# A transformer block with an expert layer on one core: joined residual and norm, a square on ScalarE, half of the token matrices on GpSimd, and an earlier end of the mixing-in

## The chip, the cores and the metric

The kernel runs on one core of a Trainium2 chip, in one launch. The metric is the device time in microseconds. A core has five engines with queues of their own: TensorE (PE, matrix products into PSUM; PEld are its weight loads), VectorE (DVE), ScalarE (ACT), GpSimd (POOL) and SyncE (SP), which issues most DMAs. An engine runs its instructions in the order of its queue.

## The reference, cut to what matters

256 tokens of width 1024, all in f32, go through two blocks. Three places matter here: the two ends of sublayers in the first block, where a normed sum is added to x and x is normed again, and the expert layer of the second.

```python
# first block
x = x + _rms_norm(merged @ w_out[l], g_post_mix[l])
h2 = _rms_norm(x, g_pre_mlp[l])
m = jnp.square(jax.nn.relu(h2 @ w_up[l])) @ w_down[l]
x = x + _rms_norm(m, g_post_mlp[l])
# second block: starts with h = rms_norm(x, norm1_g); ends with
x = x + peer(rms_norm(x, norm2_g), w_query, sub_keys, expert_u, expert_v)
# peer, per token: 8 heads pick 16 of 16384 experts each, e = 128 * key1 + key2, with weight g
act = jax.nn.gelu(jnp.einsum('td,thkd->thk', xb, expert_u[e]))
out = jnp.einsum('thk,thkd->td', g * act, expert_v[e])
```

## The kernel before

Each f32 weight is split into two f32r parts, `wh` and `wl` (`weights`, L113): a DMA brings a piece of 1024 columns into `raw` (L110), ScalarE copies it to `wh` (L121), VectorE or GpSimd makes `wl = raw - wh` (L127). A product is three matmuls, hi x hi, hi x lo and lo x hi (`mm3`, L170). TensorE's order is that of the program (`in_line`, L143); on the other engines a planner sets the order of issue from its own estimate of the times. `cycle` (L100, L571, L606) says from which pool the buffers of the next piece come; `ring` stays open all through, `wkx` opens in space that the first attention leaves.

`rows_product` (L278) makes a sublayer's output for the two token blocks one after the other, in two PSUM tiles `pp` of 512 columns, and then calls `done`. At the end of the mixer that is `mixed` (L601), at the end of the MLP `mlp_done` (L636). Both call `residual` (L243) and `norm_parts` (L234). `residual`: ScalarE squares and sums `pp` (L212), ten small VectorE instructions make the inverse root (`rsqrt`, L192), VectorE makes `y = pp * r * gain` (L249) and adds it to `x` in SBUF (L250). `norm_parts` does the same on `x` (L212, L192, L240) and puts off the transposes of `y` (L151), which TensorE makes some products later, when `tick` says so; their results are split by ScalarE and VectorE (`split`, L178). While the second token block goes through this, TensorE works on the first block's part of the next sublayer.

In the MLP, `up_first` (L640, token-major, then transposed) and `up_done` (L612) apply the relu on ScalarE, square on VectorE (L615, L647) and split. `down` (L619) runs one unit after the other behind the up units.

The expert layer is computed densely: 64 units of `expert_u` (`u_unit`, L979) give `acts`, the gelu of all 16384 experts' products with all tokens (`u_done`, L969), and 64 units of `expert_v` (`v_units`, L1048) sum them up. In between each value is multiplied by its token's weight. For that, `weighted` (L998) makes for each token a 128 x 128 table: `m2` (L1025) has a 1 in row j, column key2 of pick j; `m1` (L1026) has the weight of pick j in column key1; TensorE multiplies them (L1007) into `acc`, and VectorE multiplies four tokens' tables into the activations that are there already (L1014, L1017); for units still to come ScalarE lays the table down in `acts` (L1019), and `u_done` multiplies it in (L976). `weighted` is a generator. It yields after every second token; TensorE gets a token's product when five tokens' matrices have been made. It is drawn once at each of the four steps of a unit, during units 32 to 63, that is 128 times; what is left is drawn behind the last unit (L1037 to L1042). Six buffers each hold `m1` and `m2`.

Of the kernel before, what the change touches and what calls it, by code (L numbers as in the profile page):

```python
# [9 lines left out]
F32 = mybir.dt.float32  # L10
# [3 lines left out]
AF = mybir.ActivationFunctionType  # L14
OP = mybir.AluOpType
# [4 lines left out]
P = 128  # L20
S = 256
TB = 2
D = 1024
KB = 8
# [52 lines left out]
def block_kernel(ctx: ExitStack, tc: tile.TileContext, a, out, dbg=None):  # L77
    nc = tc.nc
    vec, act, pe, pool = nc.vector, nc.scalar, nc.tensor, nc.gpsimd

    const = ctx.enter_context(tc.tile_pool(name="const", bufs=1))
    small = ctx.enter_context(tc.tile_pool(name="small", bufs=4))
# [70 lines left out]
    def defer(n, f):  # L153

        late.append([n, f])
# [20 lines left out]
    squared = [None]  # L176
# [31 lines left out]
    def rstd(srcs, junk, n):  # L208

        s = small.tile([P, 2], F32, name="ssq")  # L210
        for i, src in enumerate(srcs):
            squared[0] = act.activation(junk[:, i * 512:i * 512 + src.shape[1]], src, AF.Square, scale=float(n) ** -0.5,  # L212
                                        accum_out=s[:, i:i + 1])
        return rsqrt(s[:, 0:1], s[:, 1:2] if len(srcs) > 1 else 0.0)
# [25 lines left out]
            vec.scalar_tensor_tensor(y[:, c:e], src[:, c:e], r, gain[:, c:e], op0=OP.mult, op1=OP.mult)  # L240
        defer(wait, lambda: transpose_split(y[:, :n], n // P, dsth, dstl))

    def residual(wk, x, pp, gain):  # L243

        y = xp.tile([P, D], F32, name="ny", bufs=2)
        r = rstd(pp, y, D)
        for b in range(2):
            c = slice(b * 512, (b + 1) * 512)
            vec.scalar_tensor_tensor(y[:, c], pp[b], r, gain[:, c], op0=OP.mult, op1=OP.mult)  # L249
            vec.tensor_tensor(x[:, c], x[:, c], y[:, c], op=OP.add)  # L250


    def project(*args, **kw):
# [174 lines left out]
    hh, hl = parts()  # L428
# [139 lines left out]
    b1 = ExitStack()  # L568
    wkx = b1.enter_context(tc.tile_pool(name="wkx", bufs=1, reuse_waits="tile"))
    mixed_cycle = [wkx, ring] * 4  # L570
    cycle[:] = mixed_cycle  # L571


    mh, ml = parts()
# [24 lines left out]
    gpr = gain_row(wk, "g_pre_mlp", D)  # L599

    def mixed(tb, pp):  # L601
        residual(wk, x[tb], pp, gpm)
        norm_parts(wk, x[tb], D, gpr, hh[:, tb], hl[:, tb], 1 + tb)

    rows_product(mh, ml, "w_out", mixed)
    cycle[:] = [*mixed_cycle, wk, wk]  # L606
# [5 lines left out]
    def up_done(u, p):  # L612
        r = wk.tile([P, 2, S], F32, name="mr", bufs=3)
        act.activation(r, p, AF.Relu)
        vec.tensor_tensor(r, r, r, op=OP.mult)  # L615
        mf[u] = (wk.tile([P, 2, S], F32R, name="mfh", bufs=5), wk.tile([P, 2, S], F32R, name="mfl", bufs=5))
        split(r, *mf[u])

# [15 lines left out]
    hn, hnl = parts()  # L634

    def mlp_done(tb, pp):  # L636
        residual(wk, x[tb], pp, gpo)
        norm_parts(wk, x[tb], D, g_n1, hn[:, tb], hnl[:, tb], 1 + tb)

    def up_first(b):  # L640
        mf[2 * b], mf[2 * b + 1] = ([wk.tile([P, 2, S], F32R, name=n, bufs=5) for n in ("mfh", "mfl")] for _ in range(2))

        def emit(tb, p):
            t = slice(tb * P, (tb + 1) * P)
            r = wk.tile([P, 2, S], F32, name="mr", bufs=3).rearrange("p a b -> p (a b)")
            act.activation(r, p, AF.Relu)
            vec.tensor_tensor(r, r, r, op=OP.mult)  # L647

            def f():
                q = tps([P, 4, P])  # L650
                for k in range(4):
                    turn(q[:, k, :], r[:, k * P:(k + 1) * P])
                for n in range(2):
                    split(q[:, 2 * n:2 * n + 2, :], mf[2 * b + n][0][:, :, t], mf[2 * b + n][1][:, :, t])
            defer(1 if tb else 2 + b, f)
        return emit
# [3 lines left out]
    pp = None  # L660
# [337 lines left out]
    def weighted():  # L998
        ready = []
        banks = {}  # L1000

        def products(t, m1, m2):
            j = t // 4
            if t % 4 == 0:
                banks[j] = acc([P, 4, P])
            p = banks[j]
            matmul(p[:, t % 4, :], m2, m1, True, True)  # L1007
            if t % 4 < 3:
                return
            ts = slice(4 * j, 4 * j + 4)  # L1010
            k = 2 * (gelus[0] - HALF)
            pv = p.rearrange("p t c -> p c t")
            g = acts[0][:, :, ts]
            vec.tensor_tensor(g, g, pv[:, :P // 2, :], op=OP.mult)  # L1014
            if k:
                g = acts[1][:, :k, ts]
                vec.tensor_tensor(g, g, pv[:, P // 2:P // 2 + k, :], op=OP.mult)  # L1017
            if k < P // 2:
                act.activation(acts[1][:, k:, ts], pv[:, P // 2 + k:, :], AF.Copy)  # L1019
            mixed_in[0] = j + 1  # L1020

        for t in range(S):
            m1 = ab.tile([P, P], F32, name="m1", bufs=6)
            m2 = ab.tile([P, P], F32, name="m2", bufs=6)
            vec.tensor_scalar(m2, i128, key2[:, t:t + 1], None, op0=OP.is_equal)  # L1025
            vec.tensor_scalar(m1, i128, key1[:, t:t + 1], gwt[:, t:t + 1], op0=OP.is_equal, op1=OP.mult)  # L1026
            ready.append((t, m1, m2))
            if len(ready) > 4:
                products(*ready.pop(0))
            if t % 2:  # L1030
                yield
        while ready:
            products(*ready.pop(0))
            if len(ready) % 2 == 0:
                yield

    table = weighted()  # L1037
    for u in range(HALF, NU):
        for _ in u_unit(u):
            next(table, None)  # L1040
    for _ in table:
        pass  # L1042
    abs_.close()
# [128 lines left out]
```

## Time and profile before

| | us |
|---|---|
| median of 3 runs | 1353.45 (1352.4 to 1354.31) |
| the profiled execution | 1357.89 |
| its span | 1356.1 |
| mean granted clock of TensorE | 0.988 |

| engine | busy us | share of the span |
|---|---|---|
| PE | 1310.0 | 97% |
| PEld | 1166.8 | 86% |
| DVE | 979.8 | 72% |
| ACT | 667.1 | 49% |
| POOL | 197.8 | 15% |

| stretch, us | what runs |
|---|---|
| 0 to 160 | projections, two attentions, gates |
| 160 to 230 | w_branch, w_out, residual and norm |
| 230 to 435 | MLP, residual and norm |
| 435 to 545 | second block: projections, spatial gating, attention, w_out |
| 545 to 755 | queries; first 32 units of expert_u; the choice of experts beside them |
| 755 to 996 | last 32 units of expert_u, tokens mixed in |
| 996 to 1344 | 64 units of expert_v, final norm |

The busy shares are means over stages with different limits. TensorE's gaps are found in the timeline of its instructions: the figure in brackets is its idle time before the instruction and what ended it. Granted clock 1.00 is the upper of the clock's two levels (2.4 GHz), 0.50 the lower.

### The profile page before, as it was taken

Reading aid. Unit: us, or ns where it says so; the run is one execution under the profiler, and the core shown is the slowest. Engines: PE = TensorE matmul, PEld = TensorE weight load, DVE = VectorE, ACT = ScalarE, POOL = GpSimd, SP = SyncE. Lnnn points to the kernel's source line nnn. Section 1 sums busy time; section 2 is a strip of 40 time slices with the busy share of each in tenths; the row PEclk is TensorE's granted clock in tenths of the full one; section 3 lists DMA queues with packets and bytes.
Section 4 is the critical chain, followed back from the end, with each engine's and each line's share of the span. In section 5 each row is a group of like instructions: output and inputs, shape, how many; then the busy total and the mean of one; then the engine's idle time right before and its main releaser. Section 6 shows DMA issues by size and latency. Waiting matters only on the chain.

```text
span 1356.1 us, 22115 instructions
## 1 busy us (share of the span) xinstructions
PE 1310.0 (97%) x8324; PEld 1166.8 (86%) x8324; DVE 979.8 (72%) x2255; ACT 667.1 (49%) x1018; POOL 197.8 (15%) x103
## 2 busy tenths in 40 slices
PE   6999898999998999999999999999989999999997
PEld 5788896799986777999999999999978888888886
DVE  6676678555568795699995799999965555555555
ACT  5576644544444655455554444434434445444543
POOL 2221223322235235400000000000000000000001
PEclk9999898999998999999999999999989999999999
DMA  7453464666544424456666544444456666666662
GB/s 283 161 177 120 142 216 134 207 188 189 190 156 155 144 90 163 133 150 182 203 197 198 163 143 149 144 142 140 141 177 195 190 196 194 195 191 195 193 194 84
DMA packets 64187, 230.61 MB, mean 170 GB/s; under 512 B 7280, under 2 KB 7696, under 8 KB 63952
## 3 DMA queue, kind: packets, MB, share of 16 engines
q1 hardware_dynamic: 61632, 221.03, 52.6%
q0 software_dynamic: 1728, 6.07, 1.2%
q10 hardware_dynamic: 720, 2.10, 0.4%
q8 instruction: 65, 1.06, 0.3%
q14 instruction: 42, 0.34, 0.1%
HBM read 227.07 MB, written 2.10 MB: 169 GB/s over the span
## 4 chain that ended last, share of the span: by engine, by line
PE 80%; DVE 13%; issue 2%; ACT 2%; DMA 1%; SPq 0%; POOL 0%; ACTq 0%; DVEq 0%
PE acc L141 52%; PE mid L141 27%; DVE wl L127 4%; PE tps L151 2%; ACT wh L121 1%; DMA x<-in_x_dram 1%; DVE eq L902 1%; DVE ef L904 1%; PE tps L141 1%; DVE x L250 1%; DVE eq L899 1%; DVE at_s L346 1%; DVE tk_w L821 0%; DVE ny L240 0%; ACT ny L212 0%
## 5 line engine op out<-in xcount | busy, mean ns | idle before, releaser
L121 ACT ACTIVATE wh<-raw 128x1024 fp32r<-128x1024 f32 (+2 forms) x422 | 439.8, 1049 | 409.3 <-PE mid L141 197.6
L127 DVE TENSOR_TENSOR wl<-raw,wh 128x1024 fp32r<-128x1024 f32 (+1 forms) x350 | 449.4, 1287 | 211.6 <-ACT wh L121 211.3
L141 PE MATMUL mid<-hh,wh 128*128 128x256 f32 x1280 | 367.8, 287 | 0.0
L141 PE MATMUL mid<-hh,wl 128*128 128x256 f32 x1280 | 356.4, 278 | 0.8 <-DVE wl L127 0.8
L141 PE MATMUL mid<-hl,wh 128*128 128x256 f32 x1280 | 356.6, 279 | 0.0
L141 PEld LDWEIGHTS mid<-hl,wh 128*128 128x128 f32 x1280 | 242.5, 189 | 0.4
L141 PEld LDWEIGHTS mid<-hh,wh 128*128 128x128 f32 x1280 | 241.1, 188 | 0.4
L141 PEld LDWEIGHTS mid<-hh,wl 128*128 128x128 f32 x1280 | 240.4, 188 | 1.0 <-DVE wl L127 1.0
L127 POOL TENSOR_TENSOR wl<-raw,wh 128x1024 fp32r<-128x1024 f32 (+3 forms) x72 | 175.4, 2447 | 343.1 <-ACT wh L121 300.8
L141 PE MATMUL acc<-wh,ah 128*128 128x512 f32 x512 | 200.5, 392 | 2.9 <-ACT ah L179 2.9
L141 PE MATMUL acc<-wl,ah 128*128 128x512 f32 x512 | 200.1, 391 | 0.0
L141 PE MATMUL acc<-wh,al 128*128 128x512 f32 x512 | 200.1, 391 | 0.0
L141 PE MATMUL acc<-wh,hh 128*128 128x512 f32 (+2 forms) x288 | 117.2, 407 | 1.3 <-ACT hh L179 1.2
L141 PEld LDWEIGHTS acc<-wh,ah 128*128 128x128 f32 x512 | 96.8, 189 | 23.3 <-ACT ah L179 3.1
L141 PE MATMUL acc<-wh,hl 128*128 128x512 f32 (+2 forms) x288 | 114.4, 397 | 1.2 <-DVE hl L180 1.1
L141 PE MATMUL acc<-wl,hh 128*128 128x512 f32 (+2 forms) x288 | 114.1, 396 | 0.7 <-POOL wl L127 0.4
L141 PEld LDWEIGHTS acc<-wh,al 128*128 128x128 f32 x512 | 96.7, 189 | 20.3 <-DVE al L180 0.2
L141 PEld LDWEIGHTS acc<-wl,ah 128*128 128x128 f32 x512 | 96.8, 189 | 20.0
L1026 DVE TENSOR_SCALAR m<-tok,key,gwt 128x128 f32<-128x128 f32 x256 | 94.7, 372 | 0.0
L179 ACT ACTIVATE ah<-acts 128x512 fp32r<-128x512 f32 x64 | 40.4, 633 | 93.0 <-PE acc L141 88.9
L180 DVE TENSOR_TENSOR al<-acts,ah 128x512 fp32r<-128x512 f32 x64 | 44.3, 693 | 52.6 <-ACT ah L179 52.6
L1025 DVE TENSOR_SCALAR m<-tok,key 128x128 f32<-128x128 f32 x256 | 79.4, 311 | 3.8 <-PE acc L141 3.0
(259 smaller groups left out, 1721.4 us busy)
## 6 DMA issues: line engine op xcount, KB each, us to landing
raw<-in_expert_u_dram SPq DMA_DIRECT2D x128, 512.0 KB, 3.8
raw<-in_expert_v_dram SPq DMA_DIRECT2D x128, 512.0 KB, 4.4
raw<-in_w_down_dram SPq DMA_DIRECT2D x32, 512.0 KB, 4.3
raw<-in_w_up_dram SPq DMA_DIRECT2D x24, 512.0 KB, 4.5
raw<-in_w_in_dram SPq DMA_DIRECT2D x20, 512.0 KB, 4.5
raw<-in_w_gate_dram SPq DMA_DIRECT2D x16, 512.0 KB, 4.2
raw<-in_w_out_dram SPq DMA_DIRECT2D x16, 512.0 KB, 4.4
raw<-in_w_in_n_dram SPq DMA_DIRECT2D x12, 512.0 KB, 4.6
```

The lines of the kernel that those rows point to most:

```text
L121: i = act.activation(h[:, :n], raw[:, :n], AF.Copy)
L127: last_split[0] = eng.tensor_tensor(l[:, :n], raw[:, :n], h[:, :n].bitcast(F32), op=OP.subtract)
L141: in_line(pe.matmul(p, x, y, start=start, stop=stop))
L151: in_line(pe.transpose(out, src, ident))
L179: turned_[0] = act.activation(h, p, AF.Copy)
L180: vec.tensor_tensor(l, p, h.bitcast(F32), op=OP.subtract)
L250: vec.tensor_tensor(x[:, c], x[:, c], y[:, c], op=OP.add)
L346: vec.tensor_scalar(s[:, cols[tb]], s[:, cols[tb]], r[:, tb:tb + 1], None, op0=OP.mult)
L899: turn_of(vec.tensor_tensor(eq, i50.unsqueeze(1).unsqueeze(1).to_broadcast(shape), posf[:, h:h + 2, :].unsqueeze(3).to_broadcast(shape), o ...
L902: vec.tensor_tensor(eq, eq, ecand[:, h:h + 2, :].unsqueeze(2).to_broadcast(shape), op=OP.mult)
L1025: vec.tensor_scalar(m2, i128, key2[:, t:t + 1], None, op0=OP.is_equal)
L1026: vec.tensor_scalar(m1, i128, key1[:, t:t + 1], gwt[:, t:t + 1], op0=OP.is_equal, op1=OP.mult)
```

## The change

- `residual` and the `norm_parts` behind it become one function, `residual_norm`. It multiplies `pp` by the gain in PSUM, makes `pp = pp * r + x` there, squares and sums that, and makes the normed `y` from `pp` and the second gain. `x` is written last, by a ScalarE copy from PSUM.
- In the MLP the square of the relu is made by ScalarE.
- `cycle` for w_branch and w_out draws `ring, ring, wkx, wkx` in place of `wkx, ring`.
- `m2` is made by GpSimd, `m1` still by VectorE.
- At every twelfth step the generator is drawn a second time, so that it ends during unit 30 of these 32.

```diff
-    def residual(wk, x, pp, gain):
+    def residual_norm(x, pp, gain, gain2, dsth, dstl, wait):
         y = xp.tile([P, D], F32, name="ny", bufs=2)
-        r = rstd(pp, y, D)
+        cs = [slice(b * 512, (b + 1) * 512) for b in range(2)]
+        def square(s, b):
+            squared[0] = act.activation(y[:, cs[b]], pp[b], AF.Square, scale=float(D) ** -0.5, accum_out=s[:, b:b + 1])
+        s = small.tile([P, 2], F32, name="ssq")
+        square(s, 0)
+        vec.tensor_tensor(pp[0], pp[0], gain[:, cs[0]], op=OP.mult)
+        square(s, 1)
+        r = rsqrt(s[:, 0:1], s[:, 1:2])
+        vec.tensor_tensor(pp[1], pp[1], gain[:, cs[1]], op=OP.mult)
+        s = small.tile([P, 2], F32, name="ssq")
         for b in range(2):
-            c = slice(b * 512, (b + 1) * 512)
-            vec.scalar_tensor_tensor(y[:, c], pp[b], r, gain[:, c], op0=OP.mult, op1=OP.mult)
-            vec.tensor_tensor(x[:, c], x[:, c], y[:, c], op=OP.add)
+            vec.scalar_tensor_tensor(pp[b], pp[b], r, x[:, cs[b]], op0=OP.mult, op1=OP.add)
+            square(s, b)
+        r = rsqrt(s[:, 0:1], s[:, 1:2])
+        for b in range(2):
+            vec.scalar_tensor_tensor(y[:, cs[b]], pp[b], r, gain2[:, cs[b]], op0=OP.mult, op1=OP.mult)
+        defer(wait, lambda: transpose_split(y, KB, dsth, dstl))
+        for b in range(2):
+            act.activation(x[:, cs[b]], pp[b], AF.Copy)
...
-    cycle[:] = mixed_cycle
+    cycle[:] = [ring, ring, wkx, wkx] * 2
...
     def mixed(tb, pp):
-        residual(wk, x[tb], pp, gpm)
-        norm_parts(wk, x[tb], D, gpr, hh[:, tb], hl[:, tb], 1 + tb)
+        residual_norm(x[tb], pp, gpm, gpr, hh[:, tb], hl[:, tb], 1 + tb)
...
     def mlp_done(tb, pp):
-        residual(wk, x[tb], pp, gpo)
-        norm_parts(wk, x[tb], D, g_n1, hn[:, tb], hnl[:, tb], 1 + tb)
+        residual_norm(x[tb], pp, gpo, g_n1, hn[:, tb], hnl[:, tb], 1 + tb)
...
         act.activation(r, p, AF.Relu)
-        vec.tensor_tensor(r, r, r, op=OP.mult)
+        act.activation(r, r, AF.Square)
...
-            vec.tensor_scalar(m2, i128, key2[:, t:t + 1], None, op0=OP.is_equal)
+            pool.tensor_scalar(m2, i128, key2[:, t:t + 1], None, op0=OP.is_equal)
             vec.tensor_scalar(m1, i128, key1[:, t:t + 1], gwt[:, t:t + 1], op0=OP.is_equal, op1=OP.mult)
...
     table = weighted()
+    steps = 0
     for u in range(HALF, NU):
         for _ in u_unit(u):
             next(table, None)
+            steps += 1
+            if steps % 12 == 0:
+                next(table, None)
     for _ in table:
         pass
```

## Rows read from the trace of the kernel before

**Rows 1.** by stretch: length, then busy us of PE, PEld, DVE, ACT, POOL; clock
```profile
760.00:988.00 228.00, 228.00 (x1981) 228.00 (x1980) 224.22 (x703) 98.95 (x184) 0.00 (x0) 1.00 0.48 143
...
1000.00:1340.00 340.00, 340.00 (x1497) 281.45 (x1497) 194.98 (x186) 164.00 (x186) 0.00 (x0) 1.00 0.62 186
```

**Rows 2.** TensorE's timeline, mixer's end: start, us, instruction, idle before it
```profile
227.80 1.94 PE L151 MATMUL tps<-ident,ny 128*128 128x128 f32 x8 [4.92 <-DVE ny L240]
...
233.89 0.40 PE L141 MATMUL acc<-wl,hh 128*128 128x512 f32 x1
```

**Rows 3.** TensorE's timeline at the MLP's end
```profile
417.46 0.63 PE L151 MATMUL tps<-ident,cnat 128*128 128x128 f32 x4 [1.23 <-DVE rs_x L201]
419.92 1.29 PE L151 MATMUL tps<-ident,ny 128*128 128x128 f32 x8 [1.83 <-DVE ny L240]
...
423.09 0.80 PE L141 MATMUL acc<-wh,hl 128*128 128x512 f32 x1 [0.81 <-DVE hl L180]
...
428.35 0.39 PE L141 MATMUL acc<-wh,hl 128*128 128x512 f32 x1
```

**Rows 4.** TensorE's timeline at the first down product
```profile
248.17 0.50 PE L141 MATMUL acc<-wh,mfl 128*128 128x512 f32 x1 [2.23 <-DVE mfl L180]
```

**Rows 5.** TensorE's timeline at the passage from expert_u to expert_v
```profile
989.55 0.83 PE L141 MATMUL acc<-m,m 128*128 128x128 f32 x6
...
992.73 0.49 PE L141 MATMUL acc<-m,m 128*128 128x128 f32 x2 [1.10 <-DVE m L1026]
996.10 0.79 PE L141 MATMUL acc<-wh,ah 128*128 128x512 f32 x1 [2.88 <-ACT ah L179]
...
1001.79 0.40 PE L141 MATMUL acc<-wl,ah 128*128 128x512 f32 x1
```

**Rows 6.** VectorE's timeline at the mixer's end
```profile
214.85 0.93 DVE L250 TENSOR_TENSOR x<-x,ny 128x512 f32<-128x512 f32 x1
215.71 3.43 DVE L127 TENSOR_TENSOR wl<-raw,wh 128x1024 fp32r<-128x1024 f32 x1
219.06 2.89 DVE L250 TENSOR_TENSOR x<-x,ny 128x512 f32<-128x512 f32 x1
```

**Rows 7.** line L250: count, then shortest, median and longest ns
```profile
L250 DVE TENSOR_TENSOR x<-x,ny x8: 679/1203/2890, 204.1 to 412.3; 128x512 f32<-128x512 f32 x8
```

**Rows 8.** GpSimd's timeline at the mixer's end
```profile
212.81 8.59 POOL L127 TENSOR_TENSOR wl<-raw,wh 128x1024 fp32r<-128x1024 f32 x3 [7.79 <-ACT wh L121]
```

**Rows 9.** VectorE's timeline at the MLP's end
```profile
410.81 4.38 DVE L250 TENSOR_TENSOR x<-x,ny 128x512 f32<-128x512 f32 x2
```

**Rows 10.** TensorE's timeline at w_branch's first product
```profile
161.28 0.39 PE L141 MATMUL acc<-oah,wh 128*128 128x256 f32 x1 [3.66 <-ACT wh L121]
```

**Rows 11.** the chain that ended last, two tokens: start, us, what
```profile
788.78 0.44 PE acc L141 x4
```

**Rows 12.** VectorE's timeline with tokens, late
```profile
988.84 0.43 DVE L1025 TENSOR_SCALAR m<-tok,key 128x128 f32<-128x128 f32 x1
989.04 0.49 DVE L1026 TENSOR_SCALAR m<-tok,key,gwt 128x128 f32<-128x128 f32 x1
989.29 0.56 DVE L1014 TENSOR_TENSOR acts<-acts,acc 128x256 f32<-128x256 f32 x1
```

**Rows 13.** GpSimd's groups by shape: count, busy us, mean ns
```profile
L127 POOL TENSOR_TENSOR wl<-raw,wh 128x576 fp32r<-128x576 f32 x2 | 2.9, 1432 | 4.9 <-ACT wh L121 4.9
...
L127 POOL TENSOR_TENSOR wl<-raw,wh 128x384 fp32r<-128x384 f32 x2 | 2.0, 1019 | 13.6 <-ACT wh L121 7.0 <-PE acc L141 6.6
```

**Rows 14.** VectorE's timeline in the second attention
```profile
459.38 0.62 DVE L346 TENSOR_SCALAR at_s<-at_s,at_r 128x256 f32<-128x256 f32 x2
...
470.39 2.74 DVE L346 TENSOR_SCALAR at_s<-at_s,at_r 128x256 f32<-128x256 f32 x2
```

**Rows 15.** GpSimd's timeline in the second attention
```profile
470.33 2.39 POOL L127 TENSOR_TENSOR wl<-raw,wh 128x1024 fp32r<-128x1024 f32 x1 [2.78 <-ACT wh L121]
```

**Rows 16.** VectorE's groups, 752 to 990 us: count, busy us, mean ns
```profile
L127 DVE TENSOR_TENSOR wl<-raw,wh 128x1024 fp32r<-128x1024 f32 x65 | 81.0, 1246 | 6.0 <-ACT wh L121 6.0
```

More of the change, by code (lines that the diff above doesn't have):

```diff
@@ L646, in emit @@
             act.activation(r, p, AF.Relu)
-            vec.tensor_tensor(r, r, r, op=OP.mult)
+            act.activation(r, r, AF.Square)
             def f():
```

## The prediction

> **What bounds the kernel now.** I read the page first, by its busy shares and its chain that ended last: TensorE is busy 97% of the span and holds 80% of the chain, most of the rest is VectorE. So an edit that only unloads another engine buys nothing where TensorE has no gap, and the question is where it has gaps. I then read the busy time by stretch, and TensorE's timeline around each gap. The stretch in which tokens are mixed in (760 to 988 us) is full: TensorE is busy 228.00 of 228.00 us at granted clock 1.00, VectorE 224.22, GpSimd nothing [rows 1]. The reader should see that taking work from VectorE shortens nothing there by itself; it can matter only at the stretch's end. The gaps that the edits touch are four: the end of the mixer's residual, 4.92 us [rows 2]; the end of the MLP's residual, three waits of 3.87 us in all [rows 3]; the first down product, 2.23 us [rows 4]; and the passage from the last expert_u unit to the first expert_v unit, 989.55 to 996.10 [rows 5]. A long gap also costs clock: behind the first, ten products of 512 columns take from 229.74 to 233.89 [rows 2], 0.41 us each, where the expert_v stretch at granted clock 1.00 has 1497 in 340.00 us, 0.23 each [rows 1]. That is the lower of the clock's two levels, 1.2 GHz in place of 2.4.
>
> **The change part by part.**
>
> *The join at the mixer's end.* The second token block's path from its sum to its transposes leaves TensorE open for 4.92 us. On it the join removes the two additions into x (L250): 0.93 and 2.89 us [rows 6]. Alone such an addition takes 0.68 [rows 7]; these are long because both inputs lie in SBUF while GpSimd runs three splits (8.59 us) [rows 8], to which I come back below. It puts in two multiplications by the gain, of the same width, so 2 x 0.68 us, though one fits ahead of the inverse root. So 3.82 - 1.36 = 2.5 us come off, and 2.4 stay open. The low clock costs 4.15 us for ten products that need 2.30, thus 1.85, and an estimated 0.6 of the 1.94 us of the transposes [rows 2]. Whether the clock still falls after 2.4 us no row decides: I count half, 1.2. That makes **-3.7 us**. Ends: -7.2, 4.92 + 2.45 but for a rest, if the split at 215.71 (3.43 us in VectorE's queue [rows 6]) falls elsewhere too; -1.5, if VectorE's order puts more splits ahead of the new steps. The copy of x moves to ScalarE behind the norm, which idles there. The accumulators are held some steps longer, but the next product that takes one stands behind transposes that wait for the same norm, so that hides it; if it fails, it costs tenths.
>
> *The join at the MLP's end.* The same edit. Here the two additions take 4.38 us [rows 9], so 3.0 come off. TensorE waits 1.23, 1.83 and 0.81 us [rows 3]; the first wait is for a rotation that stands behind the additions in VectorE's queue, so it goes as well. About 0.8 us stay: next late is the split behind the transposes. From 423.09 to 428.35 twelve products take 5.26 us where 2.76 are needed, 2.5 us of clock [rows 3]. Together 3.1 + 2.5 = 5.6; I take **-5.5 us**, between -7 and -2.
>
> *The square on ScalarE* (L615, L647). Sixteen passes of 512 columns leave VectorE. Nearly all are made two units before TensorE needs them, so nothing there. Only the wait of 2.23 us [rows 4] hangs on VectorE's order: one pass leaves its queue, 0.68 us by the row of the same width [rows 7]. **-0.6 us**, between -2.2 and +1.0 (ScalarE late instead, one weight copy ahead of the square).
>
> *The order of buffers* (`cycle`, L571). 42 pieces have been drawn before w_branch, so its first piece falls on the pool wkx under both orders, and TensorE waited for that piece: 3.66 us at 161.28 [rows 10]. The second piece now falls there too, but is needed only 24 products later. **0**, with -3 and +2.5 as ends: the wait shrinks or grows by what the issue order on ScalarE does to that copy.
>
> *30 units in place of 32.* TensorE's work is the same. It drew two tokens at each of 128 steps; now there are ten draws more. The generator ends after 130, at step 120, so two units stand between the last token and the first expert_v product. Before, six tokens are open behind the last expert_u product (three at 989.55, the last at 992.73), and the first expert_v product starts at 996.10, behind a wait of 1.10 for m and one of 2.88 for the split of the weights; the thirteen products from there run mostly at the low clock, until 1001.79 [rows 5]. Without that, six tokens take 6 x 0.22 = 1.3 us [rows 11], the first product starts at 990.9 and the fourteenth at 990.9 + 13 x 0.23 = 993.9 in place of 1001.79: 7.9 us. I take **-7.3 us**, leaving 0.6 for a hitch; ends -7.9 and -4.
>
> *One factor on GpSimd* (L1025). VectorE loses 256 x 0.20 us (start to start) [rows 12]. GpSimd gets 256 instructions in a stretch where it has none [rows 1]; its DMA issues for the final stage come behind them as they now come behind the last expert_u product. Each m2 waits for a free buffer of six, and TensorE needs it five tokens later. What must it not exceed? 1981 products in 228.00 us [rows 1], 64 to a unit with eight tokens, are 7.37 us per unit; 0.67 tokens more, at 0.22 [rows 11], make 7.5, or 0.86 us per token. No row shows this operation on GpSimd. Its two-input passes took 1.02 us for 384 columns and 1.43 for 576 [rows 13]: 2.15 ns per column and 0.19 fixed, so 0.47 us at 128 columns. Ends: 0.19, the fixed part alone, and 1.02, the nearest larger row. I take 0.47, the line through those rows, high rather than low, since there is one input only. GpSimd is then 55% busy, and the term is **0**; its end below is 0 too, since TensorE has no gap to give back.
>
> Against that speaks what the rows show of the two engines together. VectorE's pass with a scalar operand, SBUF to SBUF (L346), took 0.62 us for two, but 2.74 when GpSimd had begun an operation of 2.39 us just before: it ended behind GpSimd's [rows 14, 15]. The Trainium skill states this as a rule (SBUF — State Buffer, Who interferes with whom): GpSimd shares one pair of ports with VectorE's two-port modes and two-input passes, and who comes first locks it for a whole instruction. By that rule, the trace agrees, m1 (L1026) and the splits of expert_u now exclude m2.
>
> In rows: m1 takes 0.25 us start to start [rows 12], and the splits 2 x 1.25 us [rows 16] per 8.67 tokens, 0.29; with d for m2, a token needs d + 0.54 of what they share, if changes of hand overlap nothing. At the mixer's end GpSimd's three splits of 2.39 and the two VectorE passes between them (0.68 and 1.25 alone) took 8.59, not 9.10 [rows 7, 8, 15, 16]: a change of hand overlaps 0.25 us, which leaves d + 0.29. The limit of 0.86 is reached at d = 0.57 with the overlap, at 0.32 without. With 0.47 and the overlap it is 0.76. I expect VectorE to lose to these waits about what it gains, and TensorE to stay the bound.
>
> The Trainium skill (GPSIMD Engine Reference, 4.1 Engine selection) has GpSimd at roughly line rate for one input. By it and the fixed part, d is an estimated 0.30 us, and the sum would be the same.
>
> **The sum.** -3.7 - 5.5 - 0.6 + 0 - 7.3 + 0 = -17.1 us. The profiled execution took 1357.89 us, 1.79 of them outside its span of 1356.1; nothing outside changes, so it would take 1340.8. It lies 0.33% above the median of the three runs shown, 1353.45, from which I forecast **1336.4 us**.
>
> **The rivals.**
> (a) *The joins pay little, the passage pays.* VectorE's queue is filled in an order of its own, and splits can come in front of the new steps; then each join gives its lower end. For it: 3.43 us of split stood there [rows 6]. Against: the additions themselves are gone. -1.5 - 2 - 7.3, about 1342.7.
> (b) *GpSimd and VectorE shut each other out.* The place is the stretch with tokens, the mechanism the lock above, the point 0.86 us per token. With d = 0.47 and no overlap: 0.47 + 0.54 = 1.01, so 256 x 0.15 = 38 us more, less the 17.1: 1374, slower than before. For it: VectorE is busy 224.22 of 228.00 us [rows 1], so waits there count, and L346. Against: the overlap in the rows, VectorE's relief of 0.20 us per token, and that tokens come in pairs between which GpSimd waits for buffers.
> (c) *The passage doesn't close.* The tokens end two units earlier, but the split of the first weights (2.88 us now [rows 5]) still stands behind the last unit's gelu on ScalarE, and two thirds of the gap stay. The joins pay: about 1341.2.
> (d) *Nothing arrives*: what the seams gain is lost as waits of TensorE for m2; 1352.
>
> **How the numbers follow.** Forecast 0.52, (a) 0.17, (c) 0.11, (b) 0.14, (d) 0.06. About 0.2% (2.7 us) is what a measurement of this kernel can tell from no change. Faster: forecast, (a) and (c), less 0.01: 0.79. Same: (d) and that 0.01: 0.07. Slower: (b), 0.14. The range may leave out 2 in 10: (b) stays outside, with (d). Its low end is every gain at its end but the buffers' luck only in part, near 1328; its high end takes in (a) with 0 to 6 us of waits at the lock, 1349.
>
> **What would show it.** Right: TensorE's wait ahead of the transposes is about 2.4 us at the mixer's end and under 1 at the MLP's; the new passes take 0.7 us whatever GpSimd does; the first expert_v product follows the last expert_u product within 0.6 us, at the full clock; m2 lasts 0.3 to 0.5 us on GpSimd, a unit 7.5. Wrong: units longer than 7.5 us, TensorE waiting there for m2 or a split, L1026 far above its 0.25 (b); splits of 3 us inside the joins' path (a); a wait for the weights' split at the passage (c).

## The result

| | before | changed |
|---|---|---|
| median, us | 1353.64 (1352.4 to 1354.31, 4 runs) | 1334.16 (1332.48 to 1335.88, 4 runs) |
| ratio of the two | | 0.9857 (95%: 0.984 to 0.9874), 19.4 us less |
| the profiled execution, its span, us | 1357.89, 1356.1 | 1335.88, 1334.1 |
| mean granted clock | 0.988 | 0.995 |

The forecast was 1336.4, so the time fell as far as forecast, and 2.2 us further. The parts of the sum did not all come from where they were expected, as the trace shows. The page of the changed kernel, its busy line and the engines' shares of the chain that ended last:

```profile
PE 1300.8 (98%) x8324; PEld 1159.9 (87%) x8324; DVE 908.5 (68%) x1983; ACT 683.5 (51%) x1042; POOL 407.7 (31%) x359
...
PE 88%; DVE 6%; issue 3%; ACT 1%; DMA 1%; POOL 1%; SPq 0%; POOLq 0%; ACTq 0%; DVEq 0%
```

TensorE is busy 9.2 us less, though it makes the same products: at the lower clock a product is longer, and from 545 to 744 us the products of before follow one another more slowly, as the last section shows. Its share of the chain rises from 80% to 88%.

TensorE's timeline of the changed kernel at the places of rows 10, 2, 4, 3 and 5 (start, us, instruction, idle before it and what ended it):

```profile
158.83 0.39 PE L141 MATMUL acc<-oah,wh 128*128 128x256 f32 x1 [1.42 <-ACT wh L121]
...
208.87 0.50 PE L141 MATMUL acc<-wh,hh 128*128 128x512 f32 x1 [1.26 <-ACT hh L179]
...
220.83 1.03 PE L151 MATMUL tps<-ident,ny 128*128 128x128 f32 x8
222.17 0.50 PE L141 MATMUL acc<-wh,hh 128*128 128x512 f32 x1 [0.30 <-ACT hh L179]
...
237.86 0.50 PE L141 MATMUL acc<-wh,mfl 128*128 128x512 f32 x1 [0.98 <-DVE mfl L180]
...
394.57 0.50 PE L141 MATMUL acc<-wh,hh 128*128 128x512 f32 x1 [0.76 <-ACT hh L179]
...
407.41 0.63 PE L151 MATMUL tps<-ident,ny 128*128 128x128 f32 x4 [0.44 <-DVE ny L264]
409.09 0.66 PE L151 MATMUL tps<-ident,ny 128*128 128x128 f32 x4 [1.06 <-ACT qT L410]
...
976.88 0.40 PE L141 MATMUL acc<-wh,ah 128*128 128x512 f32 x1
...
979.84 0.39 PE L141 MATMUL acc<-wl,ah 128*128 128x512 f32 x1
```

Read each row against the same product of before. At w_branch's first product the changed kernel is 161.28 - 158.83 = 2.45 us ahead [rows 10], at the first down product 248.17 - 237.86 = 10.31 [rows 4], at the first expert_v product 996.10 - 976.88 = 19.22, and at the fourteenth 1001.79 - 979.84 = 21.95 [rows 5]; from there on it is constant. These leads are the ledger of the whole study: every run below was laid beside before product by product, and "a stretch gives x" means that the lead grows by x over it.

| stretch | term of the prediction | changed kernel | parts alone |
|---|---|---|---|
| start to w_out (206) | order, 0 | 2.9, of it 0.5 before the change begins | e2: 3.0, of it 0.6 as well; untouched kernels 0.4 to 2.5 |
| w_out to the down products (206 to 260) | join -3.7, square -0.6 | 7.4 | joins: 3.1 (e1), 3.4 (e5); square: 1.2 (e10), with the joins 4.0 |
| MLP's end (400 to 440) | join -5.5 | 4.1 | 4.1 (e1, e5) |
| 440 to 545 | none | 1.6 lost | 0 (e1, e5) |
| 545 to 744 | none | 2.0 | 0.7 to 3.2 in the twelve other kernels, none of which touches it |
| 744 to the fourteenth expert_v product | units and m2, -7.3 | 7.3 | both: 8.2 (e3); units: 5.1 (e4); m2: 4.4 (e9); untouched kernels 0 to 0.8 |
| sum | -17.1 | 22.0 | |

The line 545 to 744 is not the change's. The profiled execution of before made its products there at a slightly slower pace, as the section at the end shows; its 1357.89 us lies above every other run of that kernel. It is 4.25 us above the median of before, and the profiled execution of the changed kernel is 1.72 above its own, which is about what the line 440 to 545 lost. The difference of the two, 2.5, is why the spans give 22.0 us and the medians 19.5. Each trace is one execution, and the last column says how far untouched kernels differ, so a single line is known to a microsecond or two.

### The profile page after: what moved, and what is told of

It is laid out like the page before. It is cut to its first block, busy times and chain, and to the rows that moved or that the text cites. A ratio compares the mean times of both kernels' runs of the same rounds, so it can differ in the third digit from the quotient of the medians.

```text
span 1334.1 us, 22359 instructions
## 1 busy us (share of the span) xinstructions
PE 1300.8 (98%) x8324; PEld 1159.9 (87%) x8324; DVE 908.5 (68%) x1983; ACT 683.5 (51%) x1042; POOL 407.7 (31%) x359
## 4 chain that ended last, share of the span: by engine, by line
PE 88%; DVE 6%; issue 3%; ACT 1%; DMA 1%; POOL 1%; SPq 0%; POOLq 0%; ACTq 0%; DVEq 0%
PE acc L141 51%; PE mid L141 35%; DVE wl L127 2%; PE tps L151 2%; DMA x<-in_x_dram 1%; POOL wl L127 1%; PE tps L141 1%; ACT wh L121 0%; DVE ma L605 0%; DVE rope_t L334 0%; DVE at_s L363 0%; DVE cnat L336 0%; DVE ny L240 0%; DVE hl L180 0%; DVE rope_t L335 0%
## 5 line engine op out<-in xcount | busy, mean ns | idle before, releaser
L1040 POOL TENSOR_SCALAR m<-tok,key 128x128 f32<-128x128 f32 x256 | 208.8, 831 | 211.0 <-ACT key L938 121.6
L1099 POOL TENSOR_TENSOR hh<-hh,hl 128x512 f32<-128x512 f32 x4 | 5.1, 1286 | 344.9 <-ACT hl L1098 344.9
L1041 DVE TENSOR_SCALAR m<-tok,key,gwt 128x128 f32<-128x128 f32 x256 | 84.3, 356 | 31.5 <-PE acc L141 31.5
```

Source lines behind the costliest of these rows:

```text
L1040: pool.tensor_scalar(m2, i128, key2[:, t:t + 1], None, op0=OP.is_equal)
L1099: pool.tensor_tensor(y[:, tb, c], y[:, tb, c], gfin[:, c], op=OP.mult)
```

## The experiments

**The joins alone (e1).** The kernel before with `residual_norm` in place of `residual` and `norm_parts`, nothing else.

> The kernel before, with the two joins alone. Theory S, read off the trace after: the joins stand by themselves. The MLP's first product starts about 7 us earlier (its 4.92 us of idle and the low clock behind it are gone), the second block's first attention product another 2.5 us, not 5.5, since the copies of x on ScalarE now stand ahead of splits; 9.5 us less in all, 1344. Theory P, the prediction's sizes: 3.7 us at the mixer's end and 5.5 at the MLP's, 9.2 in all, 1344 as well, but split the other way. Rival L: the mixer's end gained 7 only because another order of buffers had put other splits into VectorE's queue; alone it gains 2 to 4, and the whole 4.5 to 6.5, 1347 to 1349.

Measured: 1347.71 us, ratio 0.9944 (0.9929 to 0.996), 7.6 us less; the medians alone, against 1353.67 for before, give 6.0. In the trace it gives 3.1 us at the mixer's end and 4.1 at the MLP's. The prediction's 3.7 and 5.5 are nearer than theory S's 7 and 2.5: four microseconds at the mixer's end must come from another part. L's time is met; whether the order of buffers is the cause, as it says, e5 decides.

**The order of buffers alone (e2).**

```diff
-    cycle[:] = mixed_cycle
+    cycle[:] = [ring, ring, wkx, wkx] * 2
```

> The kernel before, with the other order of buffers for w_branch and w_out alone. Theory S: the wait of 3.66 us for w_branch's first split weights shrinks to about 1.4 us, and TensorE keeps its clock behind it, since one weight copy no longer blocks ScalarE ahead of the gates; 5 us less by the third w_branch unit, of which about half is given back at waits for splits in w_branch and w_out: 2 to 3 us less at the mixer's end, and in all 1351. Theory P, the prediction's: 0, within 1 us. Rival: the shorter wait came from the joins or from chance in the arrival of a transfer, and the wait is 3 us or more here too.

Measured: 1353.97 us, ratio 1.0004 (0.9995 to 1.0012): nothing. Three rows of TensorE's timeline show where the shorter wait goes:

```profile
158.67 0.39 PE L141 MATMUL acc<-oah,wh 128*128 128x256 f32 x1 [1.42 <-ACT wh L121]
...
169.52 0.38 PE L141 MATMUL acc<-oah,wh 128*128 128x256 f32 x1 [1.17 <-DVE ma L586]
...
208.13 1.32 PE L151 MATMUL tps<-ident,ny 128*128 128x128 f32 x8 [1.52 <-DVE ny L240]
```

The wait of 3.66 us [rows 10] is down to 1.42 here too, so it was not chance. The lead over before grows to 5.6 us by 169, and two waits of a length that before does not have there, 1.17 and 1.52 us, take most of it again: 2.3 us are left at the down products, no more than untouched kernels have there (1.7 to 3.2). Theory S had the shorter wait right and the total wrong; the prediction had the total right, though its lower end of -3 did come about for a while.

**m2 on GpSimd and 30 units (e3), 30 units with m2 on VectorE (e4), m2 on GpSimd with 32 units (e9).** They split the token part in two.

> The kernel before, with m2 on GpSimd and 30 units, the joins, the square and the order of buffers as before. Theory S and the prediction's steps alike: 7.3 to 7.9 us less, all of it at the passage from the last expert_u unit to the first expert_v unit, whose first products run at the full clock; TensorE is busy all through the stretch with tokens; 1346. Rival: the tokens cost some tenths of a us per unit by waits for m2, which the joins' earlier start had hidden; 3 to 5 us less, 1349 to 1350.

> The kernel before, with 30 units in place of 32 and m2 still on VectorE. It asks whether GpSimd's help was needed. VectorE is busy 224.2 us of 228 in the stretch with tokens; 30 units ask it for the same work in 15 us less. Theory N, needed: VectorE falls behind, by up to 224 - 213 = 11 us, TensorE waits for matrices or for the split of weights and loses what the passage gains, or more; between 3 us less and 4 us more than before. Theory U, not needed: the work that VectorE has there beside tokens (the splits of weights and activations) moves past the end of the tokens, where VectorE has two units of room, so the passage closes all the same and 6 to 8 us come off, as with GpSimd.

> The kernel before, with m2 on GpSimd alone, in 32 units. With 30 units the helper was worth 3.1 us in the trace (e3 against e4), by TensorE's waits for matrices of VectorE. Theory Z: in 32 units TensorE is full all the same, and at the passage it waits for the split of the first weights, which stands behind the last gelu and not behind matrices; 0, within 1.5 us of the kernel before, and the passage keeps its wait of 2.9 us. Rival W: VectorE, freed of 0.20 us per token, is ahead at the passage, the waits of 0.30 and 1.10 us for matrices go, and 2 to 3 us come off.

Measured, in times: e3 1343.58 us, 0.9927 (0.9913 to 0.9942), 9.9 less; e4 1348.73, 0.9962 (0.9948 to 0.9977), 5.1 less; e9 1349.86, 0.997 (0.9957 to 0.9982), 4.1 less. In the trace e3 gives 8.2 us over the passage, so its rival of 3 to 5 falls. TensorE's waits for VectorE in e4, inside the stretch with tokens, and its wait at the passage in e9:

```profile
932.84 0.49 PE L141 MATMUL acc<-m,m 128*128 128x128 f32 x2 [0.49 <-DVE m L1026]
954.48 0.49 PE L141 MATMUL acc<-m,m 128*128 128x128 f32 x2 [0.51 <-DVE m L1026]
959.19 0.49 PE L141 MATMUL acc<-m,m 128*128 128x128 f32 x2 [0.58 <-DVE m L1026]
```

```profile
990.11 0.50 PE L141 MATMUL acc<-wh,ah 128*128 128x512 f32 x1 [2.34 <-ACT ah L179]
```

With 30 units on VectorE alone the passage closes as well, but VectorE cannot keep up with eight tokens a unit: three waits, 1.58 us, and products of late tokens around them that follow one another more slowly. Beside e3 it loses 3.1 us in the stretch. Between theories N and U it lies nearer to U. With m2 on GpSimd and 32 units the waits of 0.30 and 1.10 us for matrices at the passage are gone and 2.34 of the 2.88 us stay [rows 5], so rival W is right: GpSimd pays by itself, at the passage, not in the stretch. Its 2 to 3 us were too few, since it left out the clock, which stayed at its upper level behind the 2.34 us. The first expert_v products (length, busy us of PE, PEld, DVE, ACT, POOL, granted clock), before and then e9:

```profile
996.00:1002.00 6.00, 5.90 (x14) 4.60 (x15) 1.29 (x2) 0.94 (x3) 0.00 (x0) 0.52 0.57 216
```

```profile
990.00:996.00 6.00, 5.83 (x24) 4.54 (x25) 2.68 (x4) 1.64 (x3) 0.00 (x0) 1.00 0.78 312
```

Of the 5.0 us that e9 gains over the passage itself, 1.9 are idle time, 0.8 the last tokens' products, and 2.3 this clock. In the times the two edits add up, 5.1 and 4.1 alone and 9.9 together, within intervals of about two microseconds each way; in the traces 5.1 and 4.4 alone stand against 8.2.

**The square back on VectorE in the changed kernel (e5), the square on ScalarE alone (e10).**

```diff
-        act.activation(r, r, AF.Square)
+        vec.tensor_tensor(r, r, r, op=OP.mult)
```

> The changed kernel, with the square of the MLP's relu back on VectorE. The joins alone (e1) took 3.1 us off around the mixer's end, where the changed kernel takes 7.4 off. Theory Y: the difference is the square. With it on VectorE the transposes and the first MLP products wait 0.37 and 0.89 us, the first down product 2.2 us in place of 0.98, and the clock falls behind that wait, 1.5 us more; so 3 to 4.5 us more than the changed kernel, 1337 to 1339. Theory P, the prediction's: the square is worth 0.6 us, 1335. Rival O: the difference is the order of buffers, which e1 did not have; then this kernel keeps the whole 7.4 but for 0.6, 1335 too, and the first down product waits 1 to 1.6 us without loss of clock.

> The kernel before, with the square on ScalarE alone. In the changed kernel it was worth 4.0 us around the mixer's end by the trace (against e5). Theory Y: that worth hangs on the joins. Alone, the 4.92 us ahead of the transposes stay and so does the low clock behind them; only the wait of 2.23 us at the first down product shrinks to about 1; 1 to 1.5 us less, 1352. Rival A: the parts add, and 3.5 to 4 us come off alone too, 1349.5. Theory P, the prediction's term: 0.6 us less, and nothing at the transposes.

Measured: e5 1336.04 us, 0.9863 (0.9846 to 0.9879); e10 1352.93, 0.9996 (0.9986 to 1.0006). The medians of e5 and the changed kernel are 1.9 us apart, and their runs overlap; the traces, one execution each, show where they differ. Between w_out and the down products e5 gives 3.4 us, the changed kernel 7.4, though e5 has the new order of buffers: rival O falls. TensorE's waits in e5 are e1's own, as theory Y said, and the long VectorE row below is the reason for the first two. TensorE, then VectorE in e5:

```profile
221.25 1.28 PE L151 MATMUL tps<-ident,ny 128*128 128x128 f32 x8 [0.37 <-DVE ny L264]
223.42 0.50 PE L141 MATMUL acc<-wh,hh 128*128 128x512 f32 x1 [0.89 <-ACT hh L179]
...
240.42 0.80 PE L141 MATMUL acc<-wh,mfl 128*128 128x512 f32 x1 [2.19 <-DVE mfl L180]
```

```profile
217.49 0.14 DVE L203 TENSOR_SCALAR rs_z<-rs_y 128x1 f32<-128x1 f32 x1
217.55 2.40 DVE L662 TENSOR_TENSOR mr<-mr 128x512 f32<-128x512 f32 x1
219.87 0.20 DVE L204 TENSOR_SCALAR rs_t<-rs_t 128x1 f32<-128x1 f32 x1
```

The square stands between two steps of the join's own inverse root, and there it lasts 2.40 us, not 0.68: both its inputs lie in SBUF, and GpSimd runs four splits from 210.23 on (11.95 us). This is rows 6 over again, in a new place. In the kernel before no square stood in that inverse root. Alone (e10) the edit left the wait ahead of the transposes at 5.47 us (4.92 in rows 2) and only shortened the one at the first down product to 0.98, as theory Y said; in the trace that is 1.2 us, in the times 0.6, which the interval does not tell from nothing.

With the joins the four microseconds are of three kinds: 1.4 at the transposes and the wait behind them, 1.2 for the shorter wait at the first down product (0.98 in place of 2.19), and 1.4 of clock behind that wait. For in e1 and e5 the clock, which no longer falls at the transposes, falls here, where before kept it behind the same wait of 2.23 us [rows 4]. The products behind that wait, before and then e5:

```profile
248.00:252.00 4.00, 3.83 (x17) 3.11 (x18) 0.54 (x2) 1.45 (x2) 1.42 (x1) 1.00 0.85 307
```

```profile
240.00:244.00 4.00, 3.58 (x10) 2.89 (x11) 0.79 (x3) 1.44 (x2) 0.28 (x1) 0.57 0.97 384
```

So the square is worth about a microsecond without the joins and four with them, by these traces. Whether the clock falls there in every execution was not measured.

**Where the copy of x goes: on VectorE (e6), on ScalarE but behind the splits (e12).**

```diff
-            act.activation(x[:, cs[b]], pp[b], AF.Copy)
+            vec.tensor_copy(x[:, cs[b]], pp[b])
```

```diff
-        defer(wait, lambda: transpose_split(y, KB, dsth, dstl))
-        for b in range(2):
-            act.activation(x[:, cs[b]], pp[b], AF.Copy)
+        def turned():
+            transpose_split(y, KB, dsth, dstl)
+            for b in range(2):
+                after(turned_[0], act.activation(x[:, cs[b]], pp[b], AF.Copy))
+        defer(wait, turned)
```

> The changed kernel, with the copy of x back to SBUF made by VectorE in place of ScalarE, right behind the normed y. Theory X: what the MLP's join failed to give (4.1 us in place of 5.5), and the new waits at both joins for ScalarE's splits (1.26 and 0.30 us at the mixer's end; 0.76, 0.34 and 1.06 at the MLP's), come from these copies, which stand ahead of the splits and of a rotation's copy in ScalarE's queue. Without them 2 to 3 us come off, 1331 to 1332. Rival V: the copies delay VectorE's own half of the splits and the second token block's chain by their 1.4 us; then the waits move to VectorE and the time stays within 1 us of the changed kernel, or grows by up to 2.

> The changed kernel, with the copies of x still on ScalarE but issued behind the splits of the transposes, not behind the normed y. It takes up again what e6 left open: whether the copies' place is what costs, without moving work to VectorE. Theory X: at the mixer's end the wait of 1.26 us falls to about 0.4 (as in e6) and the 0.30 goes; at the MLP's end 0.76 and 0.34 fall to about 0.5 together, and the 1.06 for the rotation's copy goes to 0 to 0.3; 2 to 2.5 us less than the changed kernel, 1332. Rival H: the copies now hold the four accumulators until after the splits, and the first product of the next sublayer, which takes one of them, waits for the copy instead, 0.6 to 1.2 us at each of the four places; within 1 us of the changed kernel.

Measured: e6 1335.52 us, 0.9857 (0.984 to 0.9873); e12 1333.16, 0.9857 (0.984 to 0.9873). Neither can be told from the changed kernel. In the changed kernel the copy stands ahead of the rotation's copy in ScalarE's queue:

```profile
407.30 1.26 ACT L267 ACTIVATE x<-acc 128x512 f32<-128x512 f32 x2 [5.15 <-DVE ny L264]
408.45 0.59 ACT L410 ACTIVATE qT<-tps 128x512 f32<-128x512 f32 x1
```

TensorE's wait at the MLP's end in e6, and at both ends in e12:

```profile
411.61 0.50 PE L141 MATMUL acc<-wh,hl 128*128 128x512 f32 x1 [2.31 <-DVE hl L180]
```

```profile
209.14 0.50 PE L141 MATMUL acc<-wh,hh 128*128 128x512 f32 x1 [1.37 <-ACT x L268]
...
395.39 0.50 PE L141 MATMUL acc<-wh,hh 128*128 128x512 f32 x1 [1.37 <-ACT x L268]
```

With the copy on VectorE the waits at the mixer's end do fall as theory X said (0.39 and 0.30 us), but at the MLP's end TensorE waits 2.31 us for the other half of the split, and the clock falls behind it. Behind the splits the copy holds the accumulators and the next products wait 1.37 us for it, twice. Rivals V and H are right: in each of the three places a wait of a microsecond or more comes with the copy. What a kernel without the copy would take was not measured.

**Twelve tokens a unit (e7), and the same with m1 made once (e8).** These ask how much room GpSimd has.

```diff
-            if steps % 12 == 0:
+            if steps % 2 == 0:
```

> The changed kernel, with an extra draw at every second step: twelve tokens per unit in place of eight (and some), done in 21 units. TensorE's own work for a unit is then 5.6 + 12 x 0.22 = 8.25 us, 0.69 us per token. It asks where GpSimd becomes the bound. Theory G: at the pace that it showed in unbroken runs in the changed kernel, 0.80 to 0.83 us per m2, its wait on VectorE included; tokens then take 256 x 0.81 = 207 us in place of 176, TensorE stands still for about 30 us: 1362 to 1368. Theory K, the lock as the prediction's rows had it, with the measured 0.66 us for one m2: 0.66 + 0.29 = 0.95 us per token, 67 us more, 1400. Theory N: no bound, GpSimd waits only because VectorE is not in a hurry; within 3 us of the changed kernel.

> As the run before, but m1 is made once, for token 0, and all tokens use it: VectorE leaves out 255 instructions (the tables that come out are not the tokens' own). It asks what an m2 costs without VectorE's m1 beside it. Theory H: m2's 0.80 us holds 0.14 to 0.2 us of waiting for m1; without it the pace is 0.60 to 0.68 us, just within TensorE's 0.69, and the time falls back to within 5 us of the changed kernel. Rival I: 0.80 us is GpSimd's own pace (its instruction and its issue), m1 has nothing to do with it; TensorE waits as in the run before, 1362 to 1368.

Measured, one run each: e7 1351.52 us, e8 1344.16. GpSimd's one group from 760 to 920 us (count, busy us, mean ns, idle) in the changed kernel, in e7 and in e8:

```profile
L1040 POOL TENSOR_SCALAR m<-tok,key 128x128 f32<-128x128 f32 x184 | 149.6, 828 | 10.6 <-PE acc L141 9.7
```

```profile
L1040 POOL TENSOR_SCALAR m<-tok,key 128x128 f32<-128x128 f32 x212 | 161.4, 780 | 0.0
```

```profile
L1041 POOL TENSOR_SCALAR m<-tok,key 128x128 f32<-128x128 f32 x219 | 160.3, 751 | 0.0
```

In e7 and e8 GpSimd is never idle, so its pace is the limit: 160 / 212 = 0.755 us per token with m1 beside it, 160 / 219 = 0.731 without. All of the stated times missed. K's 0.95 is far off, G's 0.81 holds for the changed kernel and not for this one, as shown below, and N had no bound. H thought that m1 holds m2 up by 0.14 to 0.2 us; it is 0.02, so e8's rival was right that m1 has next to nothing to do with it, and wrong on the pace. What holds m2 up is seen in e7, GpSimd first, then VectorE:

```profile
801.29 1.60 POOL L1040 TENSOR_SCALAR m<-tok,key 128x128 f32<-128x128 f32 x1
...
804.05 0.60 POOL L1040 TENSOR_SCALAR m<-tok,key 128x128 f32<-128x128 f32 x1
```

```profile
801.20 1.22 DVE L127 TENSOR_TENSOR wl<-raw,wh 128x1024 fp32r<-128x1024 f32 x1
...
804.07 0.42 DVE L1041 TENSOR_SCALAR m<-tok,key,gwt 128x128 f32<-128x128 f32 x1 [0.74 <-PE acc L141]
```

An m2 that begins 0.09 us after VectorE's split of two SBUF inputs ends 0.47 us behind that split, after 1.60 us. An m2 that runs beside an m1 takes its 0.60. This is no single case: of the m2 in these 160 us of e7, the 36 that last 1.4 us or more overlap one of the 36 splits each, and all others take 0.59 to 0.73. The split itself takes 1.22 us, as long as ever [rows 16].

So the pace hangs on how many tokens share a split. VectorE's splits in the same 160 us, the changed kernel and then e7 (count, busy us, mean ns, idle):

```profile
L127 DVE TENSOR_TENSOR wl<-raw,wh 128x1024 fp32r<-128x1024 f32 x43 | 53.2, 1237 | 2.8 <-ACT wh L121 2.4
```

```profile
L127 DVE TENSOR_TENSOR wl<-raw,wh 128x1024 fp32r<-128x1024 f32 x36 | 43.9, 1219 | 0.0
```

In the changed kernel a split comes every 184 / 43 = 4.3 tokens, in e7 every 212 / 36 = 5.9. That is why G's 0.81, which is the changed kernel's pace (149.6 / 184), was too slow for e7. The changed kernel needs 160 / 184 = 0.87 us per token, and GpSimd is idle in it for 10.6 of 160 us: 7% to spare.

**The old order of buffers in the changed kernel (e11).**

> The changed kernel with the order of buffers of before. Alone (e2) the new order was worth nothing (1.0004, 0.9995 to 1.0012), though its wait for the first w_branch piece was 2.2 us shorter; the gain went again at a wait for the normed y ahead of the first token block's transposes at the mixer's end, 1.52 us, and one of 1.17 for the gated sum in w_branch. Theory F: with the joins that second wait has no cause, so in the changed kernel the order does pay, 2 to 2.5 us: without it 1336 to 1337, with 3.5 us of wait at the first w_branch product. Rival N: it pays nothing here either, the gain goes at other waits: 1334, within 1 us.

Measured: 1335.53 us, 0.9865 (0.9849 to 0.9882), between the two theories. The first w_branch product waits 3.48 us again, and up to w_out the trace gives 1.1 us less than the changed kernel's. Kernels with the same code differ there by more (0.4 to 2.5 us), so whether the order pays a microsecond or nothing stays open.

## Why the prediction was right, and where by luck

**The mixer's end, -3.7: near for the join alone** (3.1 and 3.4 in e1 and e5), **and partly by luck.** The additions left the path, and the new passes take 0.70 us each whatever GpSimd does, as stated. One saving was overlooked: the normed y read x in SBUF before, which took 2.44 us for two passes; from PSUM it takes 1.41. VectorE's rows, before then changed:

```profile
225.88 2.44 DVE L240 SCALAR_TENSOR_TENSOR ny<-x,rs_z,gain 128x512 f32<-128x512 f32 x2
```

```profile
218.21 1.41 DVE L264 SCALAR_TENSOR_TENSOR ny<-acc,rs_z,gain 128x512 f32<-128x512 f32 x2
```

The idle time ahead of the transposes is 0.37 us (e1) and 0 (changed), not the 2.4 that the prediction left open, and the clock stays up there, where it counted half. In e1 that gives 5.7 us. Two losses that were not in its sum bring them down to 3.1: 1.0 at a new wait for ScalarE's split (1.26 us, at the first token block), and 1.6 of clock, which falls at the first down product instead. Splits of VectorE still stand inside the join's inverse root, as rival (a) feared, though shorter than its 3 us: 2.01 us at 215.23 in the changed kernel, where such a split alone takes 1.25 [rows 16].

**The square, -0.6: near alone, wrong here.** The step that failed is "nearly all are made two units before TensorE needs them, so nothing there". It asked when the result is needed, not what stands behind the pass in VectorE's queue. In e1 and e5 the planner puts one into the join's inverse root, where it takes 2.40 us, and the first down product comes late enough to lose clock as well. Alone the term is 1.2 in the trace, with the joins 4.0. The prediction had this very risk at hand as rival (a), splits in front of the new steps, and had not applied it to the square. That the square left VectorE in the same change was luck for the sum.

**The MLP's end, -5.5: 4.1.** The step that failed is that the copy of x moves to ScalarE "which idles there". It stands ahead of a rotation's copy and of splits; waits of 1.06, 0.76 and 0.34 us are new. A second one: VectorE's order now has a split (1.25 us alone [rows 16]) and the next sublayer's rotation (cnat, two passes of 0.41 alone) inside the chain, both while GpSimd runs splits:

```profile
397.04 2.50 DVE L127 TENSOR_TENSOR wl<-raw,wh 128x1024 fp32r<-128x1024 f32 x1
...
402.71 2.08 DVE L336 TENSOR_TENSOR cnat<-rope_t 128x256 f32<-128x256 f32 x2
```

The low clock behind the seam [rows 3] was won back as said.

**The order of buffers, 0: right in the total** (e2), wrong in the path: the wait at w_branch did shrink by 2.2 us, and two later ones grew.

**30 units, -7.3: measured 7.3 in this trace, but not by 30 units alone.** The first expert_v product follows the last expert_u product at 0.12 us and the full clock; rival (c) is out. The prediction put all of the passage down to the units and gave the helper 0. On VectorE alone the units give 5.1 us, and the helper alone 4.1 (times). "TensorE has no gap to give back" held in the stretch and not at its end, where the last tokens' matrices were late [rows 5].

**m2, 0.47 us: it takes 0.60** (median 0.602 in e7), so the line through the two-input rows [rows 13] was too low by a quarter, and the one-input estimate of 0.30 by half. The Trainium skill's words on GpSimd (GPSIMD Engine Reference, 4.1 Engine selection), roughly line rate for one input, are not borne out for this pass: on VectorE, before, it took 0.29 (median). With 0.60 the prediction's own formula, d + 0.29 = 0.89, passes its limit of 0.86 and would have called (b). It was saved by a second error: m1 takes no part in the lock. The rule of the Trainium skill (SBUF — State Buffer, Who interferes with whom) holds here for passes with two SBUF inputs; for VectorE's one-input pass m1 the runs show no lock. L346 has one input too, and it did wait for GpSimd's split [rows 14, 15]; whether VectorE's pass or GpSimd's instruction makes the difference, no run shows. What was said on who pays is wrong too: VectorE lost nothing (m1 356 ns on average from 760 to 920 us, 348 before), GpSimd stretched. What the formula should hold is m2 start to start, 0.58 (804.05 to 804.63 in e7), and one split's hold of some 1.0 us (1.60 - 0.60), shared by the tokens between two splits. In e7 that is 0.58 + 1.0 / 5.9 = 0.75, against 0.755 measured; in the changed kernel 0.58 + 1.0 / 4.3 = 0.81, as measured there. So rival (b) stayed away by 0.05 to 0.06 us per token, not by the 0.10 that the prediction counted.

So the sum came out near although terms missed on both sides, and in that it was lucky. In the ledger, against the prediction: 3.1 us more at the mixer's end with the square, 2.9 more up to w_out (e2 and e11 leave open how much of it is the change's), 2.0 more that belong to the profiled execution of before, 1.4 less at the MLP's end, 1.6 less by the clock below; together 5.0, which is, but for rounding, the 22.0 of the spans less 17.1. In the times the joins alone (7.6) and units and m2 (9.9) make 17.5 of the 19.4 us; the square and the order, each nothing by itself, leave the rest within the intervals.

## What to carry over

When a chain of small steps on a busy engine is shortened, look at what the scheduler will now place into it: a pass of 0.7 us off the path took 2.4 us in it, and an edit worth a microsecond alone was worth four beside the other in these traces. Where a gap was closed, the clock fell behind the next wait instead, in e1 and e5; so read the granted clock there too. Price a helper engine by what holds it out, instruction by instruction (here VectorE's split of two SBUF inputs did, m1 did not), and by how often that comes in the kernel at hand: the margin was 7%. A copy that is moved to an "idle" engine is late for someone; ask which buffer it frees and which queue it heads.

## What was not expected of the hardware

Two waits of TensorE in the second block's attention, 0.4 and 0.9 us, are the same in all fourteen traces. In the profiled execution of the changed kernel, and in e8's, the clock fell behind them; in e7, whose code is the same up to there, and in the eleven others it did not. The two waits in the changed kernel:

```profile
464.56 0.30 PE L151 MATMUL tps<-ident,at_s 128*128 128x128 f32 x1 [0.37 <-DVE at_s L363]
465.75 0.55 PE L151 MATMUL tps<-ident,at_s 128*128 128x128 f32 x3 [0.89 <-DVE at_s L363]
```

The stretches from 465 to 475 us (length, busy us of PE, PEld, DVE, ACT, POOL, granted clock), changed, then e11:

```profile
465.00:470.00 5.00, 4.25 (x15) 2.72 (x17) 4.79 (x22) 1.72 (x6) 0.55 (x1) 0.78 0.18 70
470.00:475.00 5.00, 5.00 (x25) 3.45 (x24) 4.03 (x9) 4.63 (x12) 2.29 (x2) 0.88 0.00 0
```

```profile
465.00:470.00 5.00, 3.75 (x18) 2.24 (x18) 4.83 (x17) 1.57 (x5) 1.52 (x2) 1.00 0.36 108
470.00:475.00 5.00, 5.00 (x28) 3.77 (x29) 4.81 (x16) 4.97 (x12) 2.11 (x2) 1.00 0.00 0
```

That is the 1.6 us lost between 440 and 545 in the ledger. Such a gap is worth closing for its chance of the lower clock, and one execution doesn't tell its price.

TensorE's pace also differs at granted clock 1.00. From 700 to 720 us the profiled execution of before made 172 products in 20.00 busy us, and so did e6's; e2 and the changed kernel made 179. Before, then e2:

```profile
700.00:720.00 20.00, 20.00 (x172) 20.00 (x171) 18.03 (x18) 9.23 (x11) 0.00 (x0) 1.00 0.70 212
```

```profile
700.00:720.00 20.00, 20.00 (x179) 20.00 (x179) 17.46 (x17) 9.38 (x11) 0.00 (x0) 1.00 0.66 215
```

What makes the difference is not known; it comes to about 2 us from 545 to 744, in code that no edit of e2 touches. Parts of this size are told apart by several runs or by places in the trace, not by two spans.
